# A hybrid GDN/GLA layer on one core: chunk-end decays from a product on TensorE instead of a load, transfers counted longer by the order maker, and the work beside the heads in another order

## The chip, the cores and the metric

The kernel runs on one core of one Trainium2 chip. The metric is the device time of one execution in microseconds (us). TensorE (PE) does matrix products and transposes into PSUM, VectorE (DVE) and ScalarE (ACT) evacuate PSUM and do elementwise work, GpSimd (POOL) takes a share of the elementwise work, and SyncE (SP) issues every DMA transfer from one queue, in program order. Each engine runs its own instructions in order and waits on semaphores for the others.

## The reference

One layer over a sequence of 1024 frames of width 1024, float32 throughout. The part that the change touches is branch A, the gated delta rule with 8 heads of 128; branch B (gated linear attention, GLA, 4 heads), cross-attention and the MLP run before and behind it.

```python
h = rmsnorm(x);  one input projection -> GDN q,k,v,z,decay,beta; GLA q,k,v,r,gate; merge gates
# branch A, per head and chunk
gc    = cumsum(g)                                     # log decay within the chunk
decay = exp(where(incl, gc_i - gc_j, -inf))
lower = where(strict, beta_i * (k k^T) * decay, 0)
u, w  = triangular_solve(I + lower, [beta*v, beta*exp(gc)*k])
k_dec = k * exp(gc[last] - gc)                        # uses the chunk-end decay
g_end = exp(gc[last])                                 # and so does this
delta = u_c - w_c S;  o = (q exp(gc)) S + ((q k^T) decay) delta
S     = g_end * S + k_dec^T delta
# then: gated RMSNorm with silu(z), output projection, sigmoid merge of A and B,
# output projection, cross-attention to 256 memory tokens, MLP (relu squared), final RMSNorm
```

## The kernel before

All large products are made three times in fp32r, with both operands split into a high and a low part (`mm3`, lines 578, 580 and 582: hi·hi, lo·hi, hi·lo). Many of them use a seven-product form for 2 x 2 blocks (`wino`, `gla_dense`), others the plain form (`g_fm`, six lines of code around `mm3`: 48 matmuls of 128x512 for 128 output rows).

The stages follow each other: start-up and norms; GLA (from about 250 us), one head at a time; GDN (from about 680 us), the eight heads in four pairs; merge, cross-attention and MLP (from about 1105 us). The time of PE that the heads' small products leave free is filled with dense work: generators of dense products stand in a queue (`self.dense`), and the head code calls `fill(n)` to pull n matmul groups from it, or `until(name)` to pull until a named unit is done. How many groups go where is written by hand: `SFILL` for each step of the scan over chunks, `PFILL` around the first pair, `TFILL` around the later ones; which units stand in the queue for which pair is `FILL` (numbers are units of the merge gates, `z2` the output gate of GDN head 2, `Q1` and `O1` products of weights); `EXTRA` is the order of the dense units beside each GLA head (k, v, q of the GDN pair that is prepared there, `t` a gate unit).

In the GDN stage `gdn_cols` first makes, for all chunks and heads, `gge` = exp(gc[last]) and `kf` = exp(gc[last] − gc). For that it loads the last element of each chunk of `gcd` (the cumulated decays, 8 x 1024 in DRAM) to all 128 partitions:

```python
g = self.til(sq, [P, GH, NB], "gge", bufs=1)
...
nc.sync.dma_start(g, self.gcd.rearrange("h (c t) -> t h c", t=P)[P - 1:P].broadcast_to([P, GH, NB]))
nc.vector.tensor_tensor(self.kf, self.gge, self.tm[:, :, 0], SUB)
```

`self.tm` holds the same cumulated decays with time on the partitions. Then `gdn_decay` loads each head's row of `gcd` to all partitions (`dm`), masks it on POOL, subtracts and exponentiates; `gdn_keys` loads the pair's keys, transposes them on PE (`transpose4`, line 650), takes their squares on ACT (`jk`) and scales them by `kf` into `kdt` on DVE; `gdn_gram` makes k k^T (line 1358) and masks it into `NT`; `gdn_subst` inverts 32 x 32 blocks by substitution on DVE, with some steps on POOL (lines 1414 and 1416), and hands `PF` to `gdn_inverse` (line 1438); `gdn_scan` runs over the chunks.

What stands in which place on each engine in the end is set by the class `Plan`: it takes the recorded instructions with costs (`Op`), works out due times backwards (`latest`) and places the instructions forward with a list scheduler (`forward`), which can also put some elementwise products on POOL instead of DVE. A transfer counts there as 60 ns on SP, then bytes over `RATE`, then `LAND` ns. `LAYP`, `LAYQ` are the order of the tiles in two pools of the GDN stage, `EV` the place of early events of the start-up, `SOON` the time by which `gdn_inverse` is made due earlier.

Of the kernel before, what the change touches and what calls it, by code (L numbers as in the profile page):

```python
# [47 lines left out]
EV = (('K2', 1, 'x0'), ('K3', 1, 'kk'), ('V0', 4, 'x1'), ('V1', 0, 's0'), ('V1', 8, 'n0'), ('V2', 8, 's1'), ('V3', 1, 'kv'), ('V3', 4, 'n1'))  # L48
LOVU = (5,)
LOV = (0, 2, 5)  # L50

# [6 lines left out]
def bcol(t, n):  # L58
# [5 lines left out]
           "Reciprocal", "StreamTranspose", "TensorScalarAffineSelect")  # L64
ENGINES = {mybir.EngineType.PE: "tensor", mybir.EngineType.DVE: "vector", mybir.EngineType.Activation: "scalar",
           mybir.EngineType.Pool: "gpsimd", mybir.EngineType.SP: "sync"}
EXTRA = (('k', 'v', 't', 'q'), ('v', 't', 'k', 'q'), ('v', 't', 'k', 'q'), ('v', 't', 'k', 'q', 'z0'))
QB, FOLDB = 2, 1
SFILL, PFILL, TFILL = 4, (4, 12), (4, 14, 4, 10, 12, 10)
FILL = ((5, 6, 7, 8), ('Q0', 10, 'Q1', 'z6', 'Q2'), (9, 'O1', 'z3', 'Q3'), ('z2', 'z4', 'O0', 'z5', 11, 'O3', 'z7'), ('O2', 12, 13))  # L70
LASTG = (14, 15)
LAYP = (('dm', 4096, 2), ('q', 4096, 2), ('k1', 4096, 2), ('Pm', 4096, 1), ('NT0', 4096, 2), ('NT1', 4096, 2), ('k0', 4096, 2), ('kdt0', 4096, 2), ('kdt1', 4096, 2), ('pr', 1024, 1), ('PF', 8192, 1))
LAYQ = (('AT', 4096, 2), ('X', 4096, 2), ('acc', 2048, 2), ('v0', 4096, 2), ('v1', 4096, 2), ('sz', 2048, 2))
OUT = "out_0_dram"
HOLD, MARGIN = 0, 0
SOON = 40000
ROUNDS, TOP, PAD, WINDOW, LOAD, HORIZON, LAND, RATE = 1, 228656, 128, 3413, 1283, 30000, 2600, 390


def size(ap):  # L80
# [6 lines left out]
class Op:  # L87
# [7 lines left out]
    def __init__(self, ins, flex):  # L95
        eng = self.eng = ENGINES[ins.engine]
        ins_, outs = [[x for x in q if getattr(x, "bass_ap", None) is not None] for q in (ins.ins, ins.outs)]
        n = size(outs[0])
        psum = lambda x: x.bass_ap.tensor.name[:3] in ("pd_", "ps_")
        self.name, self.opcode, self.acc = ins.name, ins.opcode, []  # L100
        for w, q in enumerate((ins_, outs)):
            for x in q:
                p = x.ap[0][0]
                lows, span = [x.bass_ap.offset % p if p > 1 else x.bass_ap.offset], 0
                for st, k in sorted(x.ap[1:]):
                    if st <= span + 1 or k * len(lows) > 16:
# [12 lines left out]
        times = {"vector": (150 + scan + n * 1.042 + 60 * scalar, 85, 34, 35), "gpsimd": (290 + n * 1.98 if sums else 160 + n * 0.9, 45, 60, 35)}  # L119
        if sums and n <= 16:  # L120
            times["gpsimd"] = 430 + n * 152, 45, 60, 35
        if ins.opcode == "TensorReduce":
            times["vector"] = 420, 85, 34, 35
        if ins.opcode == "StreamTranspose":
            times["vector"] = 1880 if far else 1245, 85, 34, 35
        if ins.opcode == "Memset" and far:
            times["gpsimd"] = 450, 45, 60, 35
        self.times = {e: (d - early, early + own, early + lat) for e, (d, early, own, lat) in times.items()}
        if ins.opcode == "DMACopy":
            self.dma, self.cost, self.own, self.lat = True, 60, LAND, LAND  # L130
# [366 lines left out]
class Layer:  # L497
# [223 lines left out]
    def phase0(self, xp):  # L721
        nc, a = self.nc, self.a
        with ExitStack() as ctx:
# [461 lines left out]
    def queue_gla(self):  # L1185
# [5 lines left out]
        for h in range(LH):  # L1191
# [105 lines left out]
    def gdn_cols(self, sq):  # L1297

        nc = self.nc
        g = self.til(sq, [P, GH, NB], "gge", bufs=1)  # L1300
        k = self.til(sq, [P, GH, NB], "kf", bufs=1)
        self.gge, self.kf = (t.rearrange("p h c -> p c h") for t in (g, k))
        nc.sync.dma_start(g, self.gcd.rearrange("h (c t) -> t h c", t=P)[P - 1:P].broadcast_to([P, GH, NB]))
# [1152 lines left out]
```

## Time and profile before

| | us |
|---|---|
| median of 3 runs | 2140.47 (2139.57 to 2142.14) |
| the profiled execution | 2139.06 |
| its span | 2137.4 |
| PE busy in it | 2099.2 (98%) |
| DVE busy | 1598.8 (75%) |
| ACT busy | 1212.3 (57%) |
| POOL busy | 133.8 (6%) |

The span goes from the first instruction to the last; 1.7 us of the profiled execution's time lie around it. The mean clock of PE was 0.998 of full speed. In rows of the profile `L1358` is line 1358 of the kernel before, `out<-in` are tile names, `pd` and `ps` are PSUM tiles of dense and of head products, `x` counts instructions, and `PEld` is the load of the stationary operand. A wait row reads: engine, tile and line that waited, `<-` what ended the wait, then us in total, number of waits and the longest.

### The profile page before, as it was taken

To read this page: it belongs to the slowest core of one execution; us is meant where nothing else is said; L and a number is where in the kernel's file an instruction comes from. 1 tells how busy PE (TensorE), PEld (TensorE's weight loads), DVE (VectorE), ACT (ScalarE), POOL (GpSimd) and SP (SyncE) were. 2 spreads that over 40 slices of the span, in tenths; PEclk is the share of its full clock that TensorE was granted. 3 is DMA by queue.
4 is the path that set the end of the run, shared out by engine and by line. 5 is a ranking of instruction groups with operands and counts; after the bars stand their busy time and mean duration, and the time that the engine had idled before them with its cause. 6 is when DMAs were issued, how large, how long until landed. Compare 5 with 4: busy or idle time off the path is not lost.

```text
span 2137.4 us, 30916 instructions
## 1 busy us (share of the span) xinstructions
PE 2099.2 (98%) x10932; PEld 1781.1 (83%) x10932; DVE 1598.8 (75%) x2851; ACT 1212.3 (57%) x2396; POOL 133.8 (6%) x158
## 2 busy tenths in 40 slices
PE   8999999999999999999999999999999999999998
PEld 8889788898888888888878878888788888887787
DVE  7858888948775888887468899479967666566855
ACT  7456666637645477765555346565755556433433
POOL 0001000000001313121000000000000000000000
PEclk9999999999999999999999999999999999999999
DMA  8322222222325444644487752226444446778862
GB/s 326 129 69 62 95 99 92 81 61 94 100 94 152 148 150 139 207 158 137 145 279 243 231 182 81 97 79 207 135 155 145 154 150 205 224 250 258 257 196 100
DMA packets 166155, 329.54 MB, mean 154 GB/s; under 512 B 25192, under 2 KB 33768, under 8 KB 166000
## 3 DMA queue, kind: packets, MB, share of 16 engines
q1 hardware_dynamic: 165856, 327.53, 47.0%
q8 instruction: 86, 1.41, 0.3%
q14 instruction: 69, 0.57, 0.1%
q10 hardware_dynamic: 144, 0.03, 0.0%
HBM read 227.32 MB, written 100.17 MB: 153 GB/s over the span
## 4 chain that ended last, share of the span: by engine, by line
PE 75%; DVE 12%; DMA 7%; issue 2%; ACT 2%; SPq 1%; POOL 1%; DVEq 0%; ACTq 0%; POOLq 0%
PE pd L578 18%; PE pd L580 18%; PE pd L582 18%; PE ps L578 4%; PE ps L582 4%; PE ps L580 4%; PE ps L650 2%; DVE wop L619 2%; PE ps L1447 1%; DMA raw<-in_w_dram 1%; DMA e<-ad 1%; PE ps L1438 1%; DMA e<-obd 1%; SPq L537 1%; PE ps L1136 1%
## 5 line engine op out<-in xcount | busy, mean ns | idle before, releaser
L618 ACT ACTIVATE wop<-raw 128x512 fp32r<-128x512 f32 (+1 forms) x527 | 340.6, 652 | 350.6 <-PE pd L582 149.1
L619 DVE TENSOR_TENSOR wop<-raw,wop 128x512 fp32r<-128x512 f32 (+1 forms) x502 | 352.5, 706 | 189.2 <-ACT wop L618 185.3
L582 PE MATMUL pd<-t,wop 128*128 128x512 f32 x344 | 135.7, 394 | 0.0
L580 PE MATMUL pd<-t,wop 128*128 128x512 f32 x344 | 135.2, 393 | 0.2 <-DVE t L619 0.2
L578 PE MATMUL pd<-t,wop 128*128 128x512 f32 x344 | 134.1, 390 | 0.1
L578 PE MATMUL pd<-A1b,wop 128*128 128x512 f32 x276 | 107.8, 391 | 1.1 <-ACT wop L618 1.1
L580 PE MATMUL pd<-A1b,wop 128*128 128x512 f32 x276 | 107.6, 390 | 0.0
L582 PE MATMUL pd<-A1b,wop 128*128 128x512 f32 x264 | 103.0, 391 | 0.1
L1265 DVE SCALAR_TENSOR_TENSOR dx<-dx,convw,dx 128x1023 f32<-128x1023 f32 (+2 forms) x72 | 90.8, 1281 | 2.7 <-ACT dx L1263 2.5
L580 PE MATMUL pd<-A1a,wop 128*128 128x512 f32 x212 | 83.2, 393 | 0.0
L578 PE MATMUL pd<-A1a,wop 128*128 128x512 f32 x212 | 82.5, 389 | 0.0
L582 PE MATMUL pd<-A1a,wop 128*128 128x512 f32 x200 | 78.6, 393 | 0.0
L580 PEld LDWEIGHTS pd<-t,wop 128*128 128x128 f32 x344 | 64.6, 188 | 13.8 <-DVE t L619 0.5
L578 PEld LDWEIGHTS pd<-t,wop 128*128 128x128 f32 x344 | 64.6, 188 | 13.7 <-ACT t L618 0.6
L582 PEld LDWEIGHTS pd<-t,wop 128*128 128x128 f32 x344 | 64.6, 188 | 13.1
L618 ACT ACTIVATE whi<-raw 128x512 fp32r<-128x512 f32 x66 | 40.6, 627 | 43.4 <-PE pd L580 11.0
L578 PEld LDWEIGHTS pd<-A1b,wop 128*128 128x128 f32 x276 | 51.8, 188 | 12.3 <-ACT wop L618 1.9
L580 PEld LDWEIGHTS pd<-A1b,wop 128*128 128x128 f32 x276 | 51.8, 188 | 10.6
L582 PEld LDWEIGHTS pd<-A1b,wop 128*128 128x128 f32 x264 | 49.6, 188 | 10.7 <-DVE wop L619 0.5
L619 DVE TENSOR_TENSOR wlo<-raw,whi 128x512 fp32r<-128x512 f32 x58 | 39.5, 685 | 10.7 <-ACT whi L618 10.7
L931 ACT ACTIVATE dx<-pd 128x512 f32<-128x512 f32 x52 | 30.8, 593 | 29.4 <-PE pd L582 28.3
L578 PE MATMUL pd<-B0b,wop 128*128 128x512 f32 x112 | 43.8, 391 | 3.5 <-DVE A0b L1797 2.1
(643 smaller groups left out, 6466.7 us busy)
## 6 DMA issues: line engine op xcount, KB each, us to landing
raw<-in_w_dram SPq DMA_DIRECT2D x120, 256.0 KB, 3.5
raw<-in_w_dram SPq DMA_DIRECT2D x32, 512.0 KB, 4.0
e<-ad SPq DMA_DIRECT2D x63, 256.0 KB, 4.2
ad<-q SPq DMA_DIRECT2D x45, 256.0 KB, 2.7
rawa<-ad SPq DMA_DIRECT2D x42, 256.0 KB, 4.3
A0b<-tgd SPq DMA_DIRECT2D x32, 256.0 KB, 5.6
ad<-acc SPq DMA_DIRECT2D x30, 256.0 KB, 2.4
ad<-u SPq DMA_DIRECT2D x30, 256.0 KB, 3.1
```

The lines of the kernel that those rows point to most:

```text
L537: self.nc.sync.dma_start(dst, src)
L578: nc.tensor.matmul(out, lh, rh, start=first and i == 0, stop=False, skip_group_check=True)
L580: nc.tensor.matmul(out, lh, rl, start=False, stop=False, skip_group_check=True)
L582: nc.tensor.matmul(out, ll, rh, start=False, stop=last and i == n - 1, skip_group_check=True)
L618: nc.scalar.activation(hi, raw, AF.Copy)
L619: (lo_eng or nc.gpsimd).tensor_tensor(lo, raw, hi.bitcast(F32), SUB)
L650: self.nc.tensor.transpose(pt[:, i * P:(i + 1) * P], s, self.ident)
L931: nc.scalar.activation(dest(*b), pt, AF.Copy, scale=scale)
L1136: nc.tensor.matmul(po[:, :256], AT[:, c, :], v[:, c, :], start=True, stop=(c == 0))
L1265: self.nc.vector.scalar_tensor_tensor(y[:, d:], x[:, :T - d], cw[:, 3 - d:4 - d], y[:, d:], MUL, ADD)
L1438: nc.tensor.matmul(pt[:, i * 96:(i + 1) * 96], NT[:, u + i, :], PF[:, v + i, 0:96], start=True, stop=True)
L1447: nc.tensor.matmul(pt[0:96, i * n:(i + 1) * n], PF[:, v + i, 0:96], Z, start=True, stop=True)
```

## The change

`gdn_cols` no longer loads. It broadcasts the last row of `self.tm` to all partitions with one product: the stationary operand is the last column of the identity, repeated 128 times, the moving one is `self.tm`, 64 columns. `kf` and `gge` are then made from PSUM. The order of the two inner axes of `gge` and `kf` changes with it.

```diff
-        g = self.til(sq, [P, GH, NB], "gge", bufs=1)
-        k = self.til(sq, [P, GH, NB], "kf", bufs=1)
-        self.gge, self.kf = (t.rearrange("p h c -> p c h") for t in (g, k))
-        nc.sync.dma_start(g, self.gcd.rearrange("h (c t) -> t h c", t=P)[P - 1:P].broadcast_to([P, GH, NB]))
-        nc.vector.tensor_tensor(self.kf, self.gge, self.tm[:, :, 0], SUB)
+        g = self.gge = self.til(sq, [P, NB, GH], "gge", bufs=1)
+        k = self.kf = self.til(sq, [P, NB, GH], "kf", bufs=1)
+        pt = self.pss()
+        nc.tensor.matmul(pt[:, :NB * GH], self.ident[:, P - 1:P].broadcast_to([P, P]), self.tm[:, :, 0], start=True, stop=True)
+        last = pt[:, :NB * GH].rearrange("p (c h) -> p c h", h=GH)
+        nc.vector.tensor_tensor(k, last, self.tm[:, :, 0], SUB)
         nc.scalar.activation(k, k, AF.Exp)
-        nc.scalar.activation(g, g, AF.Exp)
+        nc.scalar.activation(g, last, AF.Exp)
```

In `Plan`, a transfer now counts 400 ns on SP and goes at a rate of 300 instead of 390, three inputs of the start-up excepted:

```diff
-            self.dma, self.cost, self.own, self.lat = True, 60, LAND, LAND
+            self.dma, self.cost, self.own, self.lat = True, ISSUE, LAND, LAND
             self.bytes = n * 4 * outs[0].ap[0][1]
+            if ins_[0].bass_ap.tensor.name in HEADIN:
+                self.bytes *= RATE / 390
...
-SOON = 40000
-ROUNDS, TOP, PAD, WINDOW, LOAD, HORIZON, LAND, RATE = 1, 228656, 128, 3413, 1283, 30000, 2600, 390
+SOON = 0
+ROUNDS, TOP, PAD, WINDOW, LOAD, HORIZON, LAND, RATE = 1, 228656, 128, 3413, 1283, 30000, 2600, 300
+ISSUE = 400
+HEADIN = ('in_memT_dram', 'in_wk_dram', 'in_wv_dram')
```

The hand-written tables change with it (`EV`, `LAYP`, `LAYQ`, `LASTG` and eight fill numbers of other stages too). The output gate of heads 0 and 1 (`z0`) leaves the GLA stage, where it was made in the seven-product form, and becomes two plain units in the GDN stage; beside GLA head 0 the GDN values come before the keys:

```diff
-EXTRA = (('k', 'v', 't', 'q'), ('v', 't', 'k', 'q'), ('v', 't', 'k', 'q'), ('v', 't', 'k', 'q', 'z0'))
+EXTRA = (('v', 'k', 't', 'q'), ('v', 't', 'k', 'q'), ('v', 't', 'k', 'q'), ('v', 't', 'k', 'q'))
-SFILL, PFILL, TFILL = 4, (4, 12), (4, 14, 4, 10, 12, 10)
-FILL = ((5, 6, 7, 8), ('Q0', 10, 'Q1', 'z6', 'Q2'), (9, 'O1', 'z3', 'Q3'), ('z2', 'z4', 'O0', 'z5', 11, 'O3', 'z7'), ('O2', 12, 13))
+SFILL, PFILL, TFILL = 5, (2, 12), (4, 14, 0, 8, 10, 10)
+FILL = ((7,), ('z0', 6, 10, 'z6', 'Q2'), (9, 'O1', 'z5', 'z3', 'Q3', 'z1'), ('z2', 'z4', 14, 'O0', 11, 'O3', 'z7', 8, 'Q1'), ('O2', 13, 'Q0', 12))
```

By instructions: PE has 12 more matmuls of 128x512 and the one product; 27 elementwise steps leave DVE and 17 come to POOL; SP has one issue more in all. What the order maker does with it shows at the start of the GDN stage. On SP before, the loads of pair 0's keys (`gdk`), of `gge`, of the two decay rows (`dm`), of pair 1's keys and of pair 0's queries (`gdq`):

```order
L537 DMA k_824_6131<-gdk_103 128x1024
L537 DMA k_825_6133<-gdk_103 128x1024
L1303 DMA gge_6111<-gcd 128x64x1
L1312 DMA dm_6117<-gcd 128x1024
L1312 DMA dm_6124<-gcd 128x1024
L537 DMA k_914_6474<-gdk_107 128x1024
L537 DMA k_915_6476<-gdk_107 128x1024
L537 DMA q_6470<-gdq_104 128x1024
L537 DMA q_6472<-gdq_104 128x1024
```

And the same place on SP now, where line numbers are four or five higher (`tgd` is a store of a merge gate):

```order
L1045 DMA gdq_116<-dx_5934 128x512 x2
L541 DMA k_811_6000<-gdk_103 128x1024
L541 DMA k_812_6002<-gdk_103 128x1024
L1317 DMA dm_5986<-gcd 128x1024
L1317 DMA dm_5993<-gcd 128x1024
L541 DMA q_6314<-gdq_104 128x1024
L541 DMA q_6316<-gdq_104 128x1024
L1559 DMA tgd_126<-acc_6134 128x512
L1559 DMA tgd_126<-acc_6181 128x512
L541 DMA k_896_6318<-gdk_107 128x1024
```

`gge` is gone, and the queries go ahead of pair 1's keys. On DVE at the same place before, `kf` out of `gge`, the subtraction in `dm`, the mean squares (`vv`, `rs_t`) and the scaled keys (`kdt`):

```order
L1304 TENSOR_TENSOR kf_6112<-gge_6111,tm_196 128x8x8
L1315 TENSOR_TENSOR dm_6117<-dm_6117,tm_196 128x1024
L1315 TENSOR_TENSOR dm_6124<-dm_6124,tm_196 128x1024
L1338 TENSOR_SCALAR vv_6220<-ssk_6135 128x16
L610 TENSOR_TENSOR rs_t_6226<-rs_y_6225 128x16
L1334 TENSOR_TENSOR kdt_827_6136<-ps_6137,kf_6112 128x512
L1334 TENSOR_TENSOR kdt_827_6136<-ps_6165,kf_6112 128x512
L1334 TENSOR_TENSOR kdt_843_6183<-ps_6184,kf_6112 128x512
```

On DVE now, where `ps_5981` is the new product's tile and `wlo` a weight's low part:

```order
L1309 TENSOR_TENSOR kf_5980<-ps_5981,tm_196 128x64
L623 TENSOR_TENSOR wlo_6448<-raw_6449,whi_6447 128x512
L623 TENSOR_TENSOR wlo_6448<-raw_6453,whi_6447 128x512
L1339 TENSOR_TENSOR kdt_814_6005<-ps_6006,kf_5980 128x512
L1339 TENSOR_TENSOR kdt_814_6005<-ps_6032,kf_5980 128x512
L1320 TENSOR_TENSOR dm_5986<-dm_5986,tm_196 128x1024
L1339 TENSOR_TENSOR kdt_830_6048<-ps_6049,kf_5980 128x512
L1320 TENSOR_TENSOR dm_5993<-dm_5993,tm_196 128x1024
L1343 TENSOR_SCALAR vv_6081<-ssk_6004 128x16
L1339 TENSOR_TENSOR kdt_830_6048<-ps_6065,kf_5980 128x512
```

Two `kdt` moved ahead of `dm`, and all four ahead of `rs_t`. On PE before, the first gram products (`ps<-k`) stand in one block behind 39 dense matmuls that follow the transposes:

```order
L578 MATMUL pd_6316<-A0a_202,whi_6306 128x512
L580 MATMUL pd_6316<-A0a_202,whi_6306 128x512
L582 MATMUL pd_6316<-A0a_202,wlo_6307 128x512
L1358 MATMUL ps_6238<-k_824_6131 128x128 x4
L1358 MATMUL ps_6263<-k_824_6131 128x128 x4
L1358 MATMUL ps_6285<-k_825_6133 128x128 x4
L1358 MATMUL ps_6319<-k_825_6133 128x128 x4
```

On PE now, the last two transposes of four blocks (`ps<-ident,k`) and the first gram products:

```order
L654 MATMUL ps_6049<-ident_183,k_812_6002 128x128 x4
L654 MATMUL ps_6065<-ident_183,k_812_6002 128x128 x4
L582 MATMUL pd_6390<-A1a_204,whi_6338 128x512
L584 MATMUL pd_6390<-A1a_204,whi_6338 128x512
L1363 MATMUL ps_6099<-k_811_6000 128x128 x4
L586 MATMUL pd_6390<-A1a_204,wlo_6339 128x512
L582 MATMUL pd_6390<-A1b_5877,whi_6338 128x512
L584 MATMUL pd_6390<-A1b_5877,whi_6338 128x512
L586 MATMUL pd_6390<-A1b_5877,wlo_6339 128x512
L1363 MATMUL ps_6120<-k_811_6000 128x128 x4
```

The dense matmuls moved from between the transposes and the gram products to ahead of the transposes, and the gram products stand apart from each other.

More of the change, by code (lines that the diff above doesn't have):

```diff
@@ L40 @@
 EXB, THB, GLOV, TE = 5, 1, (0, 2, 4, 6), 1
-FA, FB, FC, FD, FE, FG, FH, FI = 19, 32, 30, 20, 48, 24, 3, 0
+FA, FB, FC, FD, FE, FG, FH, FI = 23, 31, 30, 20, 47, 24, 2, 0
 SE = ((0, 0, 0, 0, 0, 0, 0, 0), (0, 1, 0, 1, 1, 1, 0, 1), (0, 1, 0, 1, 0, 1, 0, 0))
@@ L47 @@
 HEAD = (0, 1, 2)
-EV = (('K2', 1, 'x0'), ('K3', 1, 'kk'), ('V0', 4, 'x1'), ('V1', 0, 's0'), ('V1', 8, 'n0'), ('V2', 8, 's1'), ('V3', 1, 'kv'), ('V3', 4, 'n1'))
+EV = (('K2', 1, 'x0'), ('K3', 1, 'kk'), ('V0', 4, 'x1'), ('V1', 1, 's0'), ('V1', 12, 'n0'), ('V2', 12, 's1'), ('V3', 1, 'kv'), ('V3', 4, 'n1'))
 LOVU = (5,)
@@ L66 @@
            mybir.EngineType.Pool: "gpsimd", mybir.EngineType.SP: "sync"}
-EXTRA = (('k', 'v', 't', 'q'), ('v', 't', 'k', 'q'), ('v', 't', 'k', 'q'), ('v', 't', 'k', 'q', 'z0'))
+EXTRA = (('v', 'k', 't', 'q'), ('v', 't', 'k', 'q'), ('v', 't', 'k', 'q'), ('v', 't', 'k', 'q'))
 QB, FOLDB = 2, 1
-SFILL, PFILL, TFILL = 4, (4, 12), (4, 14, 4, 10, 12, 10)
-FILL = ((5, 6, 7, 8), ('Q0', 10, 'Q1', 'z6', 'Q2'), (9, 'O1', 'z3', 'Q3'), ('z2', 'z4', 'O0', 'z5', 11, 'O3', 'z7'), ('O2', 12, 13))
-LASTG = (14, 15)
-LAYP = (('dm', 4096, 2), ('q', 4096, 2), ('k1', 4096, 2), ('Pm', 4096, 1), ('NT0', 4096, 2), ('NT1', 4096, 2), ('k0', 4096, 2), ('kdt0', 4096, 2), ('kdt1', 4096, 2), ('pr', 1024, 1), ('PF', 8192, 1))
-LAYQ = (('AT', 4096, 2), ('X', 4096, 2), ('acc', 2048, 2), ('v0', 4096, 2), ('v1', 4096, 2), ('sz', 2048, 2))
+SFILL, PFILL, TFILL = 5, (2, 12), (4, 14, 0, 8, 10, 10)
+FILL = ((7,), ('z0', 6, 10, 'z6', 'Q2'), (9, 'O1', 'z5', 'z3', 'Q3', 'z1'), ('z2', 'z4', 14, 'O0', 11, 'O3', 'z7', 8, 'Q1'), ('O2', 13, 'Q0', 12))
+LASTG = (15, 5)
+LAYP = (('PF', 8192, 1), ('k1', 4096, 2), ('NT1', 4096, 2), ('NT0', 4096, 2), ('Pm', 4096, 1), ('dm', 4096, 2), ('k0', 4096, 2), ('kdt0', 4096, 2), ('kdt1', 4096, 2), ('pr', 1024, 1), ('q', 4096, 2))
+LAYQ = (('AT', 4096, 2), ('v0', 4096, 2), ('acc', 2048, 2), ('sz', 2048, 2), ('v1', 4096, 2), ('X', 4096, 2))
 OUT = "out_0_dram"
 HOLD, MARGIN = 0, 0
-SOON = 40000
-ROUNDS, TOP, PAD, WINDOW, LOAD, HORIZON, LAND, RATE = 1, 228656, 128, 3413, 1283, 30000, 2600, 390
+SOON = 0
+ROUNDS, TOP, PAD, WINDOW, LOAD, HORIZON, LAND, RATE = 1, 228656, 128, 3413, 1283, 30000, 2600, 300
+ISSUE = 400
+HEADIN = ('in_memT_dram', 'in_wk_dram', 'in_wv_dram')
 def size(ap):
```

## Prediction

> **What bounds the kernel now.** I read the profile's page first, then the list of waits of the tensor engine, then the timeline, the chain and the windows around the longest of them. The page's busy times and the list of waits:
>
> ```profile
> PE 2099.2 (98%) x10932; PEld 1781.1 (83%) x10932; DVE 1598.8 (75%) x2851; ACT 1212.3 (57%) x2396; POOL 133.8 (6%) x158
> ...
> PE ps L1358 <- DVE kdt L1334: 4.7, 1, 4.7
> PE ps L650 <- DMA k<-gdk: 2.7, 2, 1.6
> ...
> PE ps L650 <- ACT dx L1039: 1.2, 1, 1.2
> ...
> PE ps L1438 <- ACT PF L1426: 1.1, 1, 1.1
> ```
>
> The tensor engine (PE) is the bound: 2099.2 us busy in a span of 2137.4, so 38.2 us idle. A gain comes out of those 38.2 us or out of half-clock time; all else is hidden. The longest wait beyond the start-up is the one of 4.7 us at L1358, the first gram products of the gated-delta heads. The chain of waits shows what it hangs on (start, length, what), and the SP queue's timeline shows the same place:
>
> ```profile
> 680.19 8.34 SPq L1312
> 688.62 5.18 DMA dm<-gcd
> 693.91 1.97 POOL dm L1313
> 695.90 1.22 DVE dm L1315
> 697.29 2.92 POOL rs_y L609
> 700.33 0.70 DVE kdt L1334
> 701.07 5.47 PE ps L1358 x32
> ```
>
> ```profile
> 679.69 0.45 SPq L1303 DMA_DIRECT2D gge<-gcd  x1
> 680.19 8.81 SPq L1312 DMA_DIRECT2D dm<-gcd  x2
> 689.04 0.91 SPq L537 DMA_DIRECT2D k<-gdk  x2
> ```
>
> Issuing two `dm` loads took 8.81 us, directly behind the `gge` load that the change removes. Everything behind them on SP (keys of pair 1, queries, gate weights) left after 689. On VectorE (DVE), `kf`, which needs `gge`, stands ahead of `dm` and of `kdt` in program order; `kdt` frees the four PSUM tiles that the gram products need. Is it `gge` that blocks? The eight `dm` issues by themselves, and the windows of the blocked stretch (the last three columns are PE's clock, DMA share and GB/s):
>
> ```profile
> L1312 SPq DMA_DIRECT2D dm<-gcd x8: 320/354/8336, 680.2 to 915.2; - x8
> DMA to landing us min/median/max: 10.6/10.6/10.6
> ...
> 684.00:690.00 6.00, 5.10 (x31) 4.50 (x32) 0.00 (x0) 4.09 (x23) 0.00 (x0) 1.00 0.99 67
> 701.00:706.00 5.00, 4.93 (x29) 4.93 (x30) 4.83 (x19) 1.08 (x3) 1.18 (x1) 0.66 0.86 303
> ```
>
> A `dm` issue takes 0.354 us by its median and 8.336 once. The second row is `gge`'s landing: 10.6 us for 32 KB. From 684 to 690 the DMA engines were 99% busy and moved 67 GB/s: they worked on tiny pieces (`gge` is 128 x 64 single elements, 8192 of them). That is my reason to take `gge` as the cause. From 701 to 706 PE ran at 0.66 of its clock, behind its wait.
>
> **The change, part by part.** The profiled execution took 2139.06 us (span 2137.4 and 1.7 around it), 1.4 below the median 2140.47; I make the sum against the first and carry the difference to the second. The two prices for matmuls come from a window that is full of 128x512 ones, 50.00 us for 222 of them, so 0.225 us each, and from a run of eight 128x128 ones, 0.109 each:
>
> ```profile
> 1150.00:1200.00 50.00, 50.00 (x222) 41.39 (x221) 39.92 (x65) 26.86 (x49) 0.00 (x0) 1.00 0.74 247
> ...
> 708.16 0.87 PE ps L650 x8
> ```
>
> *Matmul count.* The gate of heads 0 and 1 (`z0`) leaves the seven-product block (84 matmuls) for two plain units `z0`, `z1` (96): 12 x 0.225 = +2.7 us. The one product of 64 columns that replaces `gge` is below a 128-column one: +0.1. Nothing hides either on PE.
>
> *Value before key in GLA head 0.* The 16 transposes of that head waited 1.2 us for ScalarE's `dx` (row above, L1039). They stand behind 120 plain matmuls now instead of 26, 27 us of cover against 5.9: −1.2. Heads 1 to 3 keep 36, 33 and 26 for 51, 34 and 28; none waited before, so head 3, the shortest, can lose at most 2 x 0.225 = 0.5. I take 0.
>
> *Head start.* With `gge` gone, SP's issues of pair 0 fall to 0.3 to 0.9 us each, and `kf` comes from PSUM, long before `kdt`. I take away the gram wait (4.7), the key wait (1.6, since the plain matmuls ahead of the first key transposes, 71 or 16 us, now cover the keys' load) and the slow clock, 5.0 x (1 − 0.66) = 1.7: −8.0. What is late next is the release of the four PSUM tiles: the row `kdt` 0.70 and four squares on ScalarE for each tile. The gram products stand 4, 3 and 7 plain matmuls apart, 0.9 to 1.6 us, about the four squares' pace. Between 0 and +1.0; I take +0.5.
>
> *The first inverse.* The opposite edge. PE reaches the inverse's first product, L1438, earlier, while the VectorE chain that feeds it (evacuate, 31 substitution steps, transpose) is as long as before. Its ends:
>
> ```profile
> 684.90 1.06 PE L650 MATMUL ps<-ident,k 128*128 128x128 f32 x8 [1.60 <-DMA k<-gdk]
> ...
> 704.40 0.87 DVE L1361 SCALAR_TENSOR_TENSOR NT<-ps,nb,dm 128x128 f32<-128x128 f32 x3
> ...
> 762.90 2.14 PE ps L1438 x17
> ```
>
> From the first `NT` to L1438 it is 58.5 us, with up to 4 us in it in which VectorE itself waited for others. `NT` began 19.5 us after the first key transpose; without the blockage the same steps (16 squares on ScalarE, the POOL step of 2.92, short DVE steps) need about 11.9. So L1438 is ready 66.4 to 70.4 us after the first transpose. In the new order PE has, from there to L1438, 197 plain matmuls, 48 of half their columns and 128 passes of the 128x128 kind: 197 x 0.225 + 48 x 0.113 + 128 x 0.109 = 63.7 us. The wait is 2.7 to 6.7 instead of 1.1: +1.6 to +5.6. I take +2.7, nearer the lower end, since the waits in the chain were for `dm` and for PE, which both come earlier now.
>
> The clock's row bears on the upper end: PE's clock fell after an idle of 4.7 us, and not after 1.1. [...]
>
> *The body of the heads, 712 to 1000.* Windows (busy PE, DVE third):
>
> ```profile
> 712.00:762.00 50.00, 49.52 (x276) 42.35 (x273) 44.05 (x106) 23.85 (x60) 12.21 (x15) 1.00 0.42 127
> 762.00:774.00 12.00, 11.10 (x121) 11.10 (x121) 6.39 (x14) 11.61 (x20) 4.02 (x13) 1.00 0.17 45
> 774.00:817.00 43.00, 41.87 (x316) 39.28 (x316) 40.63 (x124) 33.18 (x116) 2.06 (x2) 1.00 0.55 173
> 817.00:840.00 23.00, 21.97 (x136) 18.85 (x134) 18.51 (x37) 17.59 (x46) 11.63 (x9) 1.00 0.55 182
> 840.00:900.00 60.00, 58.78 (x440) 53.54 (x440) 53.09 (x149) 43.60 (x131) 11.42 (x22) 1.00 0.49 158
> 900.00:960.00 60.00, 58.18 (x408) 51.53 (x407) 48.16 (x121) 40.55 (x104) 18.09 (x23) 1.00 0.51 174
> 960.00:1000.00 40.00, 39.61 (x273) 35.25 (x271) 33.51 (x87) 28.54 (x91) 6.69 (x6) 1.00 0.44 143
> ```
>
> PE is idle 0.48 + 0.90 + 1.13 + 1.03 + 1.22 + 1.82 + 0.39 = 7.0 us there, 5.9 without L1438's own. The 96 plain matmuls of `z0` and `z1` are 21.6 us of new cover in this stage, laid mostly between the second and third inverse (236 instead of 147). But the third to fourth inverse loses 27 (6.1 us), and from the third pair's gram products to its inverse 14 go (3.2 us). Best: −5.9. Worst: +9.3. I take −2.5, under half of what is idle.
>
> *Transfers counted longer.* SP's order changes in pairs of neighbours almost everywhere, and by some dozens of places in the last MLP product. Idle there and in the earlier dense part:
>
> ```profile
> 1257.00:1265.00 8.00, 6.26 (x24) 4.27 (x24) 8.00 (x15) 4.74 (x9) 0.00 (x0) 1.00 0.92 317
> 1950.00:2000.00 50.00, 46.71 (x204) 37.53 (x203) 36.78 (x59) 20.02 (x35) 3.83 (x3) 1.00 0.79 251
> ```
>
> 3.3 us idle in the last one is the bound of a gain, as much again of a loss: ±3.3, I take 0.
>
> Sum: +2.7 + 0.1 − 1.2 − 8.0 + 0.5 + 2.7 − 2.5 = −5.7 us: 2133.4 against the profiled execution, 2134.8 against the median. About 0.2% (4.3 us) is what a measurement of this kernel can tell from no change.
>
> **The rivals.**
>
> *Slower: the later inverses lose their cover.* Between the third and fourth inverse VectorE's substitution becomes the bound, with the 27 + 14 matmuls fewer ahead of it: +9.3 instead of −2.5, so −5.7 + 11.8 = +6.1, 2146.6. For it: 53.09 of 60 us busy on DVE from 840 to 900. Against it: 48.16 of 60 and 33.51 of 40 after that, which leaves 18 us of room. It decides from a loss of 3.2 us in the body on.
>
> *Faster by more.* Everything falls under the new cover: L1438 waits no longer than before (0 for +2.7) and the body's 5.9 us go. −5.7 − 2.7 − 3.4 = −11.8: 2128.7. For it: the 21.6 us laid in; against it: the cover sum of 63.7 us, which is short of 66.4.
>
> *POOL holds VectorE.* Seventeen steps more go to POOL, among them two of the eight scalings of the values:
>
> ```profile
> 693.91 1.96 POOL L1313 TENSOR_SCALAR_AFFINE_SELECT dm<-dm 128x1024 f32<-128x1024 f32 x1 [0.25 <-DMA dm<-gcd]
> ...
> L1313 POOL TENSOR_SCALAR_AFFINE_SELECT dm<-dm x8: 1092/1099/1956, 692.6 to 919.9; 128x1024 f32<-128x1024 f32 x8
> ...
> 693.69 1.23 DVE L1315 TENSOR_TENSOR dm<-dm,tm 128x1024 f32<-128x1024 f32 x1 [3.12 <-POOL dm L1313]
> ...
> L1082 POOL TENSOR_TENSOR ex<-ex 128x1024 f32<-128x1024 f32 x1 | 2.3, 2264 | 10.3 <-DVE ex L864 10.3
> ```
>
> The select that began 0.22 us into a VectorE product of two SBUF operands took 1.96 instead of 1.10 us: one held the other. If two value scalings, at 2.26 us by the nearest POOL row, hold the substitution on DVE in turn, that is +4.5: −1.2 in all, 2139.3. [...]
>
> *The load was not the cause.* If `dm` blocks the queue by itself, the start keeps its waits (0 for −8.0 + 0.5 + 2.7): −0.9, 2139.6. Against it: the other `dm` issues' 0.354.
>
> **How the numbers follow.** Chances: the forecast 0.45, faster by more 0.22, slower 0.18, POOL 0.08, load not the cause 0.07. The time is the forecast's, 2134.8. Its own spread is about ±6: the two bounds at L1438 and the ±3.3 of transfers. So it lies below 2136.2 in about two thirds (0.29), the faster rival nearly always (0.21), the last two seldom (0.03): faster 0.53. Slower: five sixths of the slow rival (0.15) and 0.02 of the rest: 0.17. Same: 0.30. The range goes from 2126 (the faster rival and half of the transfers' gain) to 2146.5 (the slow rival's own time), with about 0.1 left out on each side.
>
> **What would show it.** In the new profile the longest wait of PE behind the start-up should no longer be the one for `kdt`; a `dm` issue should be under 1 us throughout; no stretch at 0.66 clock near 700; the wait for `PF` at the first inverse should have grown to 2.7 to 6.7 us and be the longest one; the transposes of GLA head 0 should wait for nothing. The prediction is wrong if `dm` is still slow to issue, if PE waits over 3 us in sum at the third and fourth inverse, or if the windows from 1250 or 1950 on lose over 3 us.

## The result: 2117.5 us, 1% faster, and half of it not where it was looked for

The changed kernel takes 2117.52 us (median of 5 runs, 2116.72 to 2119.21) against 2139.57 (5 runs, 2135.81 to 2142.14) before: ratio 0.9899, interval 0.9884 to 0.9913. That is about 22 us, where the forecast had 5.7 and its range ended at 2126. The profiled execution takes 2117.52 us with a span of 2115.8. Its page and PE's waits of 0.6 us and more (the first one stands at the start of the kernel):

```profile
span 2115.8 us, 30952 instructions
...
PE 2095.9 (99%) x10946; PEld 1783.7 (84%) x10946; DVE 1591.4 (75%) x2824; ACT 1210.2 (57%) x2390; POOL 158.3 (7%) x175
...
PE pd L582 <- ACT mT L736: 5.6, 1, 5.6
PE ps L1443 <- DVE NT L1366: 1.5, 1, 1.5
PE pd L582 <- ACT q L935: 1.4, 1, 1.4
PE ps L1443 <- ACT PF L1431: 1.3, 1, 1.3
PE pd L582 <- ACT whi L622: 0.7, 1, 0.7
```

PE was idle for 38.2 us before; now it is 2115.8 − 2095.9 = 19.9. The waits for `kdt` (4.7), for keys (2.7) and for GLA head 0's `dx` (1.2) are gone, and so are three rows from behind the heads, which stood in the list before:

```profile
PE pd L578 <- DVE A0b L1797: 2.1, 1, 2.1
PE pd L580 <- DVE B1a L619: 2.0, 3, 0.8
...
PE ps L580 <- DVE B0b L619: 1.2, 2, 0.6
```

These idle times hold 18.3 us of the gain, and the half clock near 702 another 1.7. But the span is 21.6 us shorter, with 2.8 us of products added. The other 4.4 us or so were delays that a busy time hides: a 128x512 product's row lasts 0.389 us and the next one starts 0.225 behind it in full windows (222 in 50.00 us), so PE counts as busy for 0.16 us into each wait. (Lines 578, 580 and 582 are 582, 584 and 586 now, 1358 is 1363, 1438 is 1443.)

To see where the time went I take one landmark from both traces, the first product of the merge, out of the groups of tile `B0a` (before first, then after):

```profile
L578 PE MATMUL pd<-B0a,wop x92: 389/389/389, 1092.8 to 2058.0; 128*128 128x512 f32 x92
```

```profile
L582 PE MATMUL pd<-B0a,wop x92: 389/389/389, 1082.6 to 2036.5; 128*128 128x512 f32 x92
```

The merge begins 10.2 us earlier, and the last `B0a` product comes 21.5 us earlier. So 10.2 us were gained up to the merge, though 2.8 us of products were added there, and another 11.3 behind it, in the stages that hold exactly the same products in the same order on PE. The last transposes of the GLA stage come 1.7 us earlier, so the GDN stage alone gave 8.5.

The head start looks as forecast. The decay loads' group, the first scaled keys and gram masks on DVE, and the gram products on PE:

```profile
L1317 SPq DMA_DIRECT2D dm<-gcd x8: 319/357/459, 667.6 to 906.4; - x8
```

```profile
675.23 0.69 DVE L1339 TENSOR_TENSOR kdt<-ps,kf 128x512 f32<-128x512 f32 x1 [5.38 <-ACT jk L1327]
...
685.54 4.22 DVE L1366 SCALAR_TENSOR_TENSOR NT<-ps,nb,dm 128x128 f32<-128x128 f32 x16
```

```profile
672.99 1.04 PE L654 MATMUL ps<-ident,k 128*128 128x128 f32 x8
...
676.14 1.05 PE L1363 MATMUL ps<-k 128*128 128x128 f32 x8
...
741.04 3.81 PE L1443 MATMUL ps<-PF,NT 128*128 128x96 f32 x32 [1.26 <-ACT PF L1431]
```

No `dm` issue takes over 0.459 us (8.336 before). The gram products start without a wait 3.2 us after the first transpose, where it was 16.2; `NT` begins 12.6 us after that transpose, where it was 19.5.

### The profile page after: what moved, and what is told of

It is laid out like the page before. It is cut to its first block, busy times and chain, and to the rows that moved or that the text cites. A ratio compares the mean times of both kernels' runs of the same rounds, so it can differ in the third digit from the quotient of the medians.

```text
span 2115.8 us, 30952 instructions
## 1 busy us (share of the span) xinstructions
PE 2095.9 (99%) x10946; PEld 1783.7 (84%) x10946; DVE 1591.4 (75%) x2824; ACT 1210.2 (57%) x2390; POOL 158.3 (7%) x175
## 5 line engine op out<-in xcount | busy, mean ns | idle before, releaser
L582 PE MATMUL pd<-t,wop 128*128 128x512 f32 x332 | 130.3, 393 | 0.5 <-ACT t L622 0.5
L586 PE MATMUL pd<-t,wop 128*128 128x512 f32 x332 | 130.4, 393 | 0.0
L584 PE MATMUL pd<-t,wop 128*128 128x512 f32 x332 | 130.2, 392 | 0.0
L584 PE MATMUL pd<-A1b,wop 128*128 128x512 f32 x272 | 106.3, 391 | 0.0
L582 PE MATMUL pd<-A1b,wop 128*128 128x512 f32 x272 | 105.9, 390 | 0.0
L586 PE MATMUL pd<-A1b,wop 128*128 128x512 f32 x260 | 101.2, 390 | 0.0
L584 PE MATMUL pd<-A1a,wop 128*128 128x512 f32 x208 | 81.7, 393 | 0.0
L582 PE MATMUL pd<-A1a,wop 128*128 128x512 f32 x208 | 81.4, 391 | 0.0
L586 PE MATMUL pd<-A1a,wop 128*128 128x512 f32 x196 | 76.8, 392 | 0.0
L582 PEld LDWEIGHTS pd<-t,wop 128*128 128x128 f32 x332 | 62.3, 188 | 14.0 <-ACT t L622 0.9
L584 PEld LDWEIGHTS pd<-t,wop 128*128 128x128 f32 x332 | 62.4, 188 | 13.1 <-DVE t L623 0.4
L586 PEld LDWEIGHTS pd<-t,wop 128*128 128x128 f32 x332 | 62.4, 188 | 12.8
L584 PEld LDWEIGHTS pd<-A1b,wop 128*128 128x128 f32 x272 | 51.1, 188 | 10.6 <-DVE A1b L623 0.2
L623 DVE TENSOR_TENSOR wlo<-raw,whi 128x512 fp32r<-128x512 f32 x66 | 45.2, 685 | 14.3 <-ACT whi L622 12.3
L582 PEld LDWEIGHTS pd<-A1a,wop 128*128 128x128 f32 x208 | 39.1, 188 | 8.3 <-ACT dx L935 0.3
L584 PEld LDWEIGHTS pd<-A1a,wop 128*128 128x128 f32 x208 | 39.1, 188 | 8.0
```

The costliest lines, as they stand in the source:

```text
L582: nc.tensor.matmul(out, lh, rh, start=first and i == 0, stop=False, skip_group_check=True)
L584: nc.tensor.matmul(out, lh, rl, start=False, stop=False, skip_group_check=True)
L586: nc.tensor.matmul(out, ll, rh, start=False, stop=last and i == n - 1, skip_group_check=True)
L623: (lo_eng or nc.gpsimd).tensor_tensor(lo, raw, hi.bitcast(F32), SUB)
```

## The experiments

Three things were changed together: the product (P), the counted transfers (C) and the tables (T, with `SOON` and the fill numbers). The experiments take them apart. For each I read the start of the merge (the heads' time, with all before them) and the time from there to the start of PE's last product (the late stages, with the same products in every kernel), both from the positions of PE's products in the one profiled execution of each kernel; "half clock" counts stretches of 3.41 us at half of PE's clock, from 100 us to the last product. The kernel before was measured again beside each group of experiments, with medians from 2139.57 to 2141.18, so two medians out of different groups compare to within 1 or 2 us; the ratios go by the kernel before of the same group.

| kernel | median us | ratio to before, interval | merge begins | late stages | half clock |
|---|---|---|---|---|---|
| before | 2139.57 | 1 | 1092.8 | 1036.4 | 1 |
| changed: P, C, T | 2117.52 | 0.9899, 0.9884 to 0.9913 | 1082.6 | 1025.1 | 0 |
| e1: P | 2145.13 | 1.0019, 1.0008 to 1.0031 | 1098.2 | 1035.7 | 1 |
| e2: C | 2139.54 | 0.9994, 0.9985 to 1.0003 | 1096.3 | 1033.5 | 2 |
| e9: T | 2138.83 | 0.9984, 0.9971 to 0.9996 | 1095.5 | 1036.0 | 3 |
| e8: P, C | 2140.93 | 1.0007, 0.9996 to 1.0017 | 1092.6 | 1037.1 | 3 |
| e4: P, T | 2143.41 | 1.0013, 1.0003 to 1.0022 | 1089.9 | 1043.9 | 4 |
| e3: C, T | 2127.19 | 0.9936, 0.9921 to 0.9951 | 1087.0 | 1028.6 | 1 |
| e5: C late only | 2130.14 | 0.9947, 0.9926 to 0.9968 | 1093.4 | 1029.2 | 2 |
| e6: P, T, C in the heads only | 2126.85 | 0.9929, 0.9908 to 0.9949 | 1080.4 | 1031.7 | 0 |
| e7: P, T, C late only | 2126.90 | 0.9930, 0.9909 to 0.9951 | 1095.5 | 1024.8 | 1 |
| e10: rate 390, 400 ns | 2133.68 | 0.9968, 0.9955 to 0.9980 | 1090.0 | 1035.3 | 3 |
| e11: rate 300, 60 ns | 2119.02 | 0.9902, 0.9883 to 0.9922 | 1082.0 | 1026.6 | 0 |
| e12: z0 in GLA | 2125.32 | 0.9928, 0.9911 to 0.9946 | 1083.9 | 1032.8 | 3 |
| e13: rate 390, 60 ns, landing 300 ns later | 2133.81 | 0.9972, 0.9961 to 0.9983 | 1093.3 | 1029.2 | 3 |
| e14: rate 310, 400 ns | 2117.67 | 0.9901, 0.9882 to 0.9920 | 1081.2 | 1025.9 | 1 |
| e15: rate 270, 400 ns | 2136.89 | 0.9989, 0.9979 to 0.9999 | 1087.4 | 1039.8 | 3 |
| e16: rate 250, 60 ns | 2145.27 | 1.0023, 1.0012 to 1.0035 | 1092.0 | 1042.7 | 4 |

**e1, the product alone.** Before, with `gdn_cols` of the change:

```diff
-        nc.sync.dma_start(g, self.gcd.rearrange("h (c t) -> t h c", t=P)[P - 1:P].broadcast_to([P, GH, NB]))
+        nc.tensor.matmul(pt[:, :NB * GH], self.ident[:, P - 1:P].broadcast_to([P, P]), self.tm[:, :, 0], start=True, stop=True)
```

> The kernel before with the product in place of the load, nothing else. Theory A (the load blocks SP's queue; what the product gives is the head start alone, 4.7 + 1.6 + 1.7 us, less a longer wait at the first inverse): 5 to 8 us under the kernel before, no dm issue over 1 us, the idle of PE around 1110, 1260 and 1960 as before. Theory B (dm is slow by itself): within 2 us of before, one dm issue still near 8 us.

It is slower than before. The blockage itself is gone: the `dm` group of this kernel, and then the windows of the heads behind the first inverse, of this kernel and of before.

```profile
L1313 SPq DMA_DIRECT2D dm<-gcd x8: 320/323/481, 679.1 to 909.1; - x8
```

```profile
800.00:900.00 100.00, 91.28 (x663) 82.51 (x662) 86.23 (x226) 74.00 (x223) 27.24 (x32) 0.99 0.51 166
900.00:1000.00 100.00, 96.93 (x647) 85.74 (x646) 80.22 (x195) 59.84 (x169) 24.77 (x28) 0.99 0.45 145
```

```profile
800.00:900.00 100.00, 96.61 (x697) 87.49 (x696) 88.36 (x236) 73.63 (x221) 23.05 (x30) 1.00 0.51 166
900.00:1000.00 100.00, 97.80 (x679) 86.78 (x677) 81.67 (x207) 69.09 (x195) 24.78 (x29) 1.00 0.49 161
```

The first inverse starts at 756.3, 6.6 us earlier than the 762.9 of before, close to what the forecast gave the head start. By the merge the kernel is 5.4 us later: PE is idle for 8.7 and 3.1 us in these two windows where it was 3.4 and 2.2. The idle moved behind the inverse: its waits there are for `wlo` on DVE (2.6 us in one), for keys (1.6) and for `NT` (1.3). So the cause of the blockage was right (theory B has no `dm` issue of 8 us to show), and the gain from it was wrong. The time itself lies outside of what either theory expected.

**e2, the costs alone, and e9, the tables alone.**

```diff
-            self.dma, self.cost, self.own, self.lat = True, 60, LAND, LAND
+            self.dma, self.cost, self.own, self.lat = True, ISSUE, LAND, LAND
-... HORIZON, LAND, RATE = ..., 30000, 2600, 390
+... HORIZON, LAND, RATE = ..., 30000, 2600, 300
+ISSUE = 400
```

> The kernel before with only the longer count of transfers (400 ns each on SP, rate 300). Theory A (the 11.2 us that the changed kernel gains behind the heads, at 1110, 1260 and 1960, come from the costs): about 10 us under the kernel before, those three places without idle, the 4.7 us wait for kdt still there. Theory B (they come from the tables of hand, which shift everything behind them): within 2 us of before in these places.

e9 is the changed kernel with the load of `gge` back, and 60 ns and 390:

> The changed kernel with the load back and the old costs, so the tables alone. Theory A (the parts don't add: the tables need the counted transfers and the product): merge begins 1092 to 1100 us, the late stages 1032 to 1044, time 2138 to 2150. Theory B (the tables hold the heads' gain by their 96 matmuls of cover alone): merge begins near 1083 to 1087, about 2130.

Neither gives much: e2's interval holds 1, and e9 is 0.16% faster. In e2 the heads lose 3.5 us, and the late stages gain 2.9 instead of the 10 expected. Its order also tests the blockage once more, for here a weight's load and not a `dm` stands behind `gge` on SP, and now that one is held:

```profile
679.82 0.45 SPq L1307 DMA_DIRECT2D gge<-gcd  x1
680.39 8.31 SPq L541 DMA_DIRECT2D raw<-in_w_gate_dram  x1
```

The wait for `kdt` is 1.75 us there, where the expectation kept 4.7. e9 came at 1095.5 and 1036.0, by its theory A.

**e3, the load back, and e4, the costs back**, each out of the changed kernel.

```diff
# e3
-        nc.tensor.matmul(pt[:, :NB * GH], self.ident[:, P - 1:P].broadcast_to([P, P]), self.tm[:, :, 0], start=True, stop=True)
+        nc.sync.dma_start(g, self.gcd.rearrange("h (c t) -> t h c", t=P)[P - 1:P].broadcast_to([P, GH, NB]))
# e4
-... LAND, RATE = ..., 2600, 300
-ISSUE = 400
+... LAND, RATE = ..., 2600, 390
+ISSUE = 60
```

> The changed kernel with the load of gge back in place of the product. Theory A (the load costs its 8 us at any order): 6 to 9 us over the changed kernel, a dm issue near 8 us, a long wait for kdt. Theory B (with other order and counted costs the load would be hidden): within 2 us of the changed kernel.

> The changed kernel with transfers counted as before (60 ns, rate 390, also for the three inputs). Theory A (costs make the late gain): about 10 us over the changed kernel, idle of PE back in the stages behind 1090. Theory B (the tables make it): within 2 us of the changed kernel there.

With the load back the same blockage is there again, as the groups of `dm` and `gge` show, and the kernel is slower by 9.7 us by the medians and by 7.9 by the ratios and the profiled executions (4.4 up to the merge, 3.5 behind it):

```profile
L1316 SPq DMA_DIRECT2D dm<-gcd x8: 319/364/9472, 667.8 to 911.5; - x8
...
L1307 SPq DMA_DIRECT2D gge<-gcd x1: 465/465/465, 668.3 to 668.3; - x1
```

With the costs back everything is lost, 25.9 us: 7.3 up to the merge, 18.8 behind, where theory A had about 10. So the eight combinations do not add up. From before, P loses 0.19%, C gives nothing, T gains 0.16%, P with C gives nothing, P with T loses 0.13%; C with T gains 0.64% (12.4 us by the medians), and P then 8 to 10 us more.

**e5, e6 and e7: where the costs act.** A counter taken at the start of the merge splits the transfers (e5, out of before):

```diff
+                if self.ops[-1].dma and i >= self.cut:
+                    self.ops[-1].cost, self.ops[-1].bytes = 400, self.ops[-1].bytes * RATE / 300
...
     def phase_merge(self, sp, ob):
+        if self.plan: self.plan.cut = len(self.plan.trace())
```

e6 and e7 do it in the changed kernel the other way round, 60 ns and the old rate, with `i >= self.cut` (shown) and `i < self.cut` (where the three inputs of the start-up keep their rate):

```diff
+                if self.ops[-1].dma and i >= self.cut:
+                    self.ops[-1].cost, self.ops[-1].bytes = 60, self.ops[-1].bytes * RATE / 390
```

> The kernel before, with transfers counted longer only from the merge on. Theory A (the count itself makes the late gain, by loads placed earlier in the same stage): heads as before, from the merge to the end 8 to 11 us less than before's 1036.4 us (first B0a product to the last one of PE), so about 2130. Theory B (the late stages scatter by several us with any change of the plan, the count has no steady effect): anything within 5 us of 1036.4.

> The changed kernel, with transfers counted as before from the merge on. Theory A: heads as in the changed kernel, 8 to 18 us more from the merge to the end than its 1025.1 us. Theory B: within 5 us of 1025.1 or anywhere, without relation to the count.

> The changed kernel, with transfers counted as before up to the merge and longer from there. Theory A: from the merge on 1025 to 1029 us as in the changed kernel, and the heads 7 us longer as in the kernel with all costs back. Theory B: from the merge on anything between 1025 and 1044 us.

These split the count by place. Before, with nothing but the late transfers counted longer: heads as before (1093.4), late stages 7.2 us shorter. The changed kernel with the late transfers as before: heads as in the changed kernel (1080.4), late stages 6.6 us longer. And with the heads' transfers as before: late stages as in the changed kernel (1024.8), heads 12.9 us longer. Theory A holds for the place, not for the sizes: of e5 and e6 it had expected 8 us or more behind the merge, of e7 7 in the heads. The sizes are rough, too, since the profiled execution of e6 lies 4.9 us under its median, that of e7 3.2 over and that of e5 2.3 over; by the medians e6 and e7 are 9.3 and 9.4 us slower than the changed kernel.

Part of what the count does in the heads stands at the first inverse. Product and tables with the old rate in the heads (e4, e7, e10, e13) make PE wait 4.5 to 5.1 us there, against 1.3 in the changed kernel, e6 and e11, and 1.7 in e14 (2.4 and 3.2 with the rates of 270 and 250 in e15 and e16). The row in e7:

```profile
PE ps L1445 <- ACT PF L1433: 4.5, 1, 4.5
```

Behind the merge one effect of the count shows on ScalarE, whose operand splits (`ACT B0b L618 <- DMA e<-ad`: waits for an operand's load) feed PE. Rows of its waits from the merge on, before, then in e6, then the only such row of the changed kernel among its first ones:

```profile
ACT B0b L618 <- DMA e<-ad: 13.3, 6, 4.3
...
ACT B1b L618 <- DMA e<-ad: 10.9, 7, 3.2
ACT B1b L618 <- DMA rawa<-ad: 10.3, 5, 4.3
```

```profile
ACT B1b L624 <- DMA rawa<-ad: 14.7, 5, 4.2
...
ACT B1b L624 <- DMA e<-ad: 12.4, 7, 3.5
...
ACT B0b L624 <- DMA e<-ad: 11.8, 5, 5.0
```

```profile
ACT B1b L622 <- DMA e<-ad: 5.7, 5, 1.5
```

Summed over all rows of that list from the merge to 2080, ScalarE waited 150.3 us for transfers before, 161.5 in e6, 46.0 in the changed kernel and 44.8 in e5. DVE, which follows ScalarE in order, waited 31.9, 30.7, 2.7 and 11.5. The order maker thought a load of 256 KB there in 2600 + 262144/390 = 3.27 us; by the profile's page they take 4.2 (`e<-ad`) and 4.3 (`rawa<-ad`), and the 256 KB loads of weights 3.5. So operands were asked for late and ScalarE waited for them. That PE's delays come from these waits is argued, not shown, and other kernels speak against it as the whole cause: e13 below has 137.6 us of such waits and late stages of 1029.2, e8 has 45.3 and 1037.1, and e15 has 50.9 and 1039.8. What changes with the count for certain is the order of transfers, and with it ScalarE's; PE's products stand in the same order in the late stages of the kernel before, the changed one, e6, e7, e11 and e13 to e16, so all of the difference there is delay.

**e8, product and costs with the old tables.**

> The kernel before with product and longer count, but the tables of before (z0 in the GLA stage, old fills). Theory A (the tables keep the heads' gain, which the product alone gave back behind the first inverse): merge begins no earlier than before, 1093 to 1098 us, and the late stages take 1025 to 1034, so 2130 to 2138. Theory B (the count of transfers keeps it): merge begins near 1083, about 2122.

It came as theory A has it for the heads (1092.6), but its late stages took 1037.1 us though their transfers were counted longer: PE stood at the start of the merge (2.0, 1.3, 1.0 and 0.9 us between 1105 and 1122) and lost 3.4 us in two half-clock stretches there. The count helps the late stages in most plans, not in all.

**e10 and e11: which half of the count**, out of the changed kernel:

```diff
# e10
-... LAND, RATE = ..., 2600, 300
+... LAND, RATE = ..., 2600, 390
# e11
-ISSUE = 400
+ISSUE = 60
```

> The changed kernel with the 400 ns on SP but the rate of before, 390. Theory A (it is the place of a transfer in SP's queue that was counted too short: 400 for 60 ns, with four transfers in a row 1.4 us): like the changed kernel, 2116 to 2121. Theory B (the rate makes it, 0.2 us for each 256 KB): like the kernel with old costs, over 2135.

> The changed kernel with the rate of 300 but 60 ns on SP. Theory A (the place in the queue): over 2132. Theory B (the rate): 2116 to 2121.

The rate does nearly all of it: with it alone 2119.0. The 400 ns alone give 2133.7, which neither theory had: 9.7 us less than with both old costs (e4, 2143.4), but 16 us more than with both new ones, and beside the new rate they add no more than the noise. My theory A, the place in the queue, falls as the main cause.

**e12, z0 back in the GLA stage.**

```diff
-EXTRA = (..., ('v', 't', 'k', 'q'))
+EXTRA = (..., ('v', 't', 'k', 'q', 'z0'))
-FILL = ((7,), ('z0', 6, 10, 'z6', 'Q2'), (9, 'O1', 'z5', 'z3', 'Q3', 'z1'), ...
+FILL = ((7,), (6, 10, 'z6', 'Q2'), (9, 'O1', 'z5', 'z3', 'Q3'), ...
```

> The changed kernel with the gate of heads 0 and 1 back in the GLA stage as 84 matmuls, z0 and z1 out of the GDN stage. Theory A (the 96 plain matmuls are the cover that keeps the later heads from waiting): 2.7 us less in products, 5 to 10 us more of waits of PE between 760 and 1085, so 2120 to 2126. Theory B (order alone does it, the cover was not short): 2.7 us under the changed kernel, about 2115.

2.7 us fewer products, 7.8 us slower. Up to the merge it lost only 1.3 us, net, so 4 us more of delays than the changed kernel has there (among its own are waits of 2.4 and 1.4 us at the second inverse and a stretch of 6.83 us at half clock), less than the 5 to 10 expected; 7.7 more behind the merge, with waits of 1.6 and 1.8 us and a half-clock stretch from 1110 to 1113. The 96 plain matmuls are cover, as theory A has it, but most of the loss is not where it puts it.

**e13 to e16: a line or a delay, and steady or scatter**, out of the changed kernel:

```diff
-... LAND, RATE = ..., 2600, 300
-ISSUE = 400
# e13
+... LAND, RATE = ..., 2900, 390
+ISSUE = 60
# e14
+... LAND, RATE = ..., 2600, 310
+ISSUE = 400
# e15
+... LAND, RATE = ..., 2600, 270
+ISSUE = 400
# e16
+... LAND, RATE = ..., 2600, 250
+ISSUE = 60
```

> The changed kernel with rate 390 and 60 ns, and each transfer counted as landing 300 ns later (2900 for 2600), which is more than the rate of 300 adds to a transfer of 256 KB (202 ns). Theory A (what the rate does is make transfers stand in line longer behind each other): like the kernel with old costs, over 2132. Theory B (loads were only due too late, by a constant): 2116 to 2122.

> The changed kernel with rate 310 for 300. Theory A (a steady effect of the count): 2115 to 2122. Theory B (the plan scatters, 300 is a lucky one): anything from 2117 to 2140.

> The changed kernel with rate 270 for 300. Theory A: 2113 to 2122, the late stages at most 1027 us. Theory B: anything from 2117 to 2140.

> The changed kernel with rate 250 and 60 ns on SP. Theory A: 2113 to 2124. Theory B: anything from 2117 to 2140.

A later landing at the old rate (e13) makes the late stages 1029.2 us, most of the rate's gain there, as theory B has it, but the heads stay at 1093.3, so the time is 2133.8, as theory A has it. Rate 310 is the same as 300. With 270 and 250 the gain is gone: 2136.9 and 2145.3. ScalarE's waits for transfers behind the merge stay low there (50.9 and 40.5 us in sum), and PE waits for other things, in e15 from the merge's start to the end:

```profile
PE pd L582 <- ACT wop L622: 5.8, 5, 3.1
...
PE ps L582 <- ACT B1b L622: 4.0, 2, 2.4
```

So neither theory stands whole. The effect is no steady one of "the longer, the better": e13 and e15 count a load of 256 KB alike, at 3.57 us, and their late stages differ by 10.6. It is no blind scatter either: 300 and 310 agree within 0.2 us, though their orders on SP differ, and six of the nine kernels with 300 or 310 behind the merge are under 1030 us there, all but one of those with 390 and the old landing over 1035 (e6: 1031.7). There is a fitting count near 300 to 310; between 310 and 390 nothing was tried. Why 270 fails, whether by the order of weights against operands or by chance of one plan, stays open. No version tried beats the changed kernel; e14 equals it, and e11 nearly does.

## Why the prediction was wrong, step by step

*The load blocks SP and with it the head start, −8.0 + 0.5: right as a mechanism.* e1, e3 and the changed kernel show it with the load out, in and out: longest `dm` issue 0.481, 9.472 and 0.459 us; in e2 the load holds another transfer instead. Undone in the changed kernel it is worth 8 to 10 us. But I took the gain as the edit's own, and e1 shows that it is not: with the old order and costs the edit alone is slower by 0.19%. What the edit frees is kept only if the work behind it has its loads and weights in time.

*The first inverse, a wait of 2.7 to 6.7 us: right in sum, wrong in place.* First transpose to L1443 is 741.04 − 672.99 = 68.05 us, inside the 66.4 to 70.4; the cover was 63.7, so 4.3 us of delays. Only 1.3 of them stand at L1443 itself, the others are smaller ones ahead of it (the longest idle times are 0.7 us at 700 and 0.5 at 734). That the wait stayed short there is the work of the count: it is 4.5 to 5.1 us with the rate of 390 in the heads.

To put a size on the heads' terms I sum each product's delay, which is its start behind the product before it, less the median distance for its shape in the same trace. From the end of GLA's transposes to the first inverse the delays fell from 12.4 us to 4.9. So the start and the first inverse together gave −7.6, where the forecast had −8.0 + 0.5 + 2.7 = −4.8: the rows that it named come to 9.1 us of the 12.4 (4.7, 1.6, 1.7 and 1.1), so there was more to take away, and of what is left it had 4.3 (0.5 and 3.8).

*The body, −2.5.* From the first inverse to the merge the delays fell from 25.1 us to 20.5, −4.6: inside the ends of −5.9 and +9.3. (The GDN stage's 8.5 us with 2.8 added would make 11.3 for start and body, and the delays say 12.2; they are that exact.) The second and third inverse show why, since from 800 to 900 PE did not stand at all:

```profile
800.00:900.00 100.00, 100.00 (x655) 88.95 (x654) 80.82 (x189) 63.91 (x172) 25.47 (x32) 1.00 0.46 156
900.00:1000.00 100.00, 97.91 (x725) 88.74 (x724) 81.96 (x203) 59.69 (x167) 25.51 (x34) 1.00 0.46 152
```

*Value before key, −1.2.* No wait for `dx` is left; about 1.0 us of the 1.7 up to the end of GLA came there, the other 0.7 in the start-up, which I had not priced.

*Transfers counted longer, 0 ± 3.3: this step failed.* Behind the merge 11.3 us were gained. Counting only the late transfers longer gives 7.2 of them from before (e5), and undoing only that costs 6.6 in the changed kernel (e6); in its heads the count is worth 12.9 more (e7), and without any of it the whole gain is lost, 25.9 us (e4). Two things were wrong with the step. Its bound was the idle of one window (3.3 us at 1950), though the stages behind the merge held waits at 1107 to 1119, 1257 to 1266, 1509 and 1960 to 1980, and though a busy time hides 0.16 us of each; the delays there sum to 16.7 us before and 5.4 after. The two windows that I had shown, with the same products now:

```profile
1243.00:1249.00 6.00, 6.00 (x29) 4.95 (x28) 6.00 (x11) 4.18 (x7) 0.00 (x0) 1.00 0.56 211
...
1930.00:1980.00 50.00, 50.00 (x222) 41.44 (x221) 39.15 (x63) 22.29 (x38) 3.84 (x3) 1.00 0.80 262
```

And I put it at 0, since the order changed "in pairs of neighbours": I counted how far transfers moved and not who waited for them. ScalarE's list of waits before, 150 us for transfers in these stages, could have warned that the term need not be small; how much of it reaches PE it does not tell, as e13 and e15 show. And the term was taken by itself, though the count also decides whether the head start is kept.

*The rivals.* "Slower by lost cover" did not come: the longest wait at a later inverse is 1.5 us. "POOL holds VectorE" was not tested by itself. In the GDN stage VectorE waited 16.2 us for POOL before (8.5 for `dm`, 7.7 for `rs_y`) and 9.3 in the changed kernel (8.7 of it for `rs_y`), though POOL's busy time went from 133.8 to 158.3 us. "The load was not the cause" is excluded by e1, e2 and e3. "Faster by more" had the right side and, at 2128.7, the wrong reason: its 11.8 us were all in the heads.

*Not to be settled here:* how much of the 21.5 us belongs to which part. The parts act only together, and one profiled execution of each kernel stands behind the split in heads and late stages.

## What to carry to other kernels

Where a list scheduler sets the order, its cost of a transfer is part of the kernel: compare what it counts (3.27 us here) with the landing that the profile shows (3.5 to 4.3). Then try several counts and measure each, since the best ones here, 3.45 and 3.47 us, were not the nearest to the longest landings, and 3.57 lost the gain. A bound on a change that touches every stage is the delay of all stages together, and more than the idle time shows. And a stall that is taken away is a gain only after the next chain has been checked: undo each part by itself and do each by itself, since here every part alone was worth next to nothing.

## What the runs showed of the hardware

The load of 8192 single elements (32 KB) took 10.6 us to land before and 11.4 in e3, and the issue behind it on SP took 8.34 us before, 9.47 in e3 and 8.24 in e9, where it is a `dm`, and 8.31 in e2, where it is a weight's load; in e1, e4 and the changed kernel, which have no such load, no `dm` issue took over 0.481.

PE's slow clock came in stretches of 3.41 us at 0.50 (before, from 701.57 to 704.98), or twice that (6.83 in e12), so each 3.41 us lose 1.7, and it followed waits well under 3.4 us. In e9, it followed one wait of 1.89 us that ended at 1511.5, and not one of 1.52 at 1981.6 (PE's busy time is the first column behind the comma, its clock the third from the right):

```profile
1508.57:1511.98 3.41, 1.52 (x7) 0.97 (x6) 3.41 (x6) 2.85 (x6) 0.00 (x0) 1.00 0.00 0
1511.98:1515.39 3.41, 3.41 (x10) 2.63 (x9) 3.41 (x7) 1.81 (x5) 0.00 (x0) 0.50 0.02 5
1979.60:1983.01 3.41, 1.89 (x9) 1.28 (x8) 3.41 (x5) 2.30 (x4) 2.32 (x3) 1.00 0.91 317
1983.01:1986.42 3.41, 3.39 (x15) 2.45 (x15) 3.41 (x7) 1.73 (x3) 1.09 (x1) 1.00 0.55 150
```

Single waits of 1.71 (e14), 1.72 (e2) and 2.05 us (e4) were followed by it too, while 2.58 us in e1 and 2.26 in e4 were not, and 1.3 to 1.5 us in the changed kernel were not. So the length of a wait does not tell. The 18 traces say more. Within each, the stretches start whole multiples of 3.4133 us apart, to 0.01 us (in that of before 1430.185 us, which is 419 of them), so windows of that length can be laid over the whole trace. Of the windows at full clock, from 100 us to the last product, all 15 in which PE was busy for at most 41% were followed by half clock (in before the one from 698.15, with 0.49 us busy); of those from 42 to 52%, 14 were and 8 were not (in e9 the 1.52 us from 1508.57 were, in before the 1.65 us from 694.74 were not); above that, none of over 10000 was (1.89 us from 1979.60 in e9, 1.95 us from 912.41 in the changed kernel). So as far as these traces go, half clock went with the busy share of such a window, about a half, and with it the place of a wait against the window's edge; between 42 and 52% they do not tell what decides. A stall so followed costs up to twice its length: in e14 the wait of 1.71 us and 1.7 more. The changed kernel has no such stretch up to its last product, most of those near the time before two to four.
